# A two-layer decoder trunk on one core: the last feed-forward product by quarter products, and four smaller moves ahead of it

## The chip, the cores and the metric

The kernel runs on one core of a Trainium2 chip. The core has a matrix engine (PE in the profile, with its weight loads shown as PEld), a vector engine (DVE), a scalar engine (ACT), a general engine (POOL) and a queue engine that issues DMAs (SP). Each engine works through its own queue in order and waits on semaphores of the others. The metric is the device time of one execution in microseconds (us); the time of a kernel is the median of its runs.

## The reference

The input is one sequence of 1024 tokens of width 1024. Two layers follow, each a token mixer and a squared-ReLU feed-forward block, and a last RMSNorm:

```
h = modulate(rms_norm(x, norm_mix_g[i]), sh_m, sc_m)
y = recurrent_mixer(h, ...)   if i % 2 == 0   else   pool_mixer(h, ...)
x = x + gt_m[:, None, :] * y
h = modulate(rms_norm(x, norm_ffn_g[i]), sh_f, sc_f)
u = relu(h @ w1[i]);  x = x + gt_f[:, None, :] * ((u * u) @ w2[i])
...
return rms_norm(x, final_norm_g)
```

The six vectors sh, sc and gt of a layer are one product of silu(c) with w_mod, a matrix of 1024 by 6144 for each layer. The feed-forward block is 1024 to 4096 to 1024.

## The kernel before, in words

The activations are held transposed: x[0] holds tokens 0 to 511 and x[1] tokens 512 to 1023, each as eight blocks of 128 features by 512 tokens. A float32 operand is split into a rounded part and a remainder, and a product takes three matrix instructions (`mm3`, lines 188 to 190): high by high, high by low, low by high. One such instruction has 512 columns (a token half) in nearly all of the kernel.

A remainder is made in one of two ways. `split_part` rounds on ACT and subtracts on DVE (line 181). `neg_part` rounds on ACT, negates on ACT, and lets a DMA from POOL's queue add the original on the fly (line 165); the DVE has no part in it. `prepare` does the same for the first weights `w_k` (block q of four holds six of the eight output blocks of the input projection for two of the eight input blocks): q = 0 by DVE, q = 1, 2 and 3 by DMA. The matrix instructions of that stage are on line 401, the small helper `after` on lines 325 and 328 puts its instructions in a written order on ACT, DVE and POOL.

The modulation vectors ("columns" in the following) are made off the matrix engine: a weight block mb of 512 KB is loaded, DVE multiplies it by cond and sums it (`mod_column`, line 207). `drip(n)` traces n such steps; it is called beside the weight loads of the big products, and `drip_until` where a vector is needed.

The feed-forward block goes in eight chunks of 512 hidden features. `f1` makes the squared ReLU of a chunk, `f2` or `f2_fast` multiplies it by w2. `f2_fast` treats the second product of a chunk as a two by two block product over the token halves and two halves of the features and takes seven quarter products for it where eight blocks would be needed. Its operands (t1 to t4 and three of the four u blocks) are made by DVE and ACT in `f1` with fast set; the results are spread over x by DVE (line 773), ACT (777), DVE sums (803, 807) and POOL adds (782). Product 1, 5, 6, 3 and 7 touch both token halves; products 2 and 4 touch x[1] alone. One chunk of layer 0 (chunk 6) is already taken in two visits, five products and later two, with the weight routines `f2_weights_one` and `f2_weights_two`.

The last chunk of layer 1 isn't fast: f1 without the extra operands, then `last_chunk` three times with `f2_block` (eight-block form): tokens 0 to 511, then 512 to 767, then 768 to 1023, the last two with 256 columns. Beside each the squares of finished blocks are summed (`SumSq`: ACT squares, line 262, DVE adds, line 263). `rstd_bcast` turns a sum into 1/rms for every token on all partitions: PE column sums (272), ACT root (275), DVE reciprocal and splits (276 to 280), DVE diagonals (284), PE broadcast (286). The first 512 tokens are scaled and stored by DVE (`final_norm`, 1009), the next 256 by POOL (`mid_norm`, 1024 and 1030), the last 256 by DVE behind a row form of the root (`rstd_row`, 998 to 1001).

The order of the instructions on each engine isn't the order of the text: a scheduler replays the program with its own costs and gives each engine, whenever it comes free, the ready instruction that was traced first. `issue_after` and the helper `after` tie single instructions down. Buffers of a pool are given in the order of the trace: six PSUM banks for products, two for sums, three raw weight buffers, eight split weight buffers, seven temporaries.

Of the kernel before, what the change touches and what calls it, by code (L numbers as in the profile page):

```python
# [15 lines left out]
P = 128  # L16
# [26 lines left out]
def trunk_kernel(ctx, tc, xT, vecs, wmod, w_k, w_in, w_y, w_g, w_out, w_p, w1, w2, outT):  # L43
# [200 lines left out]
    class SumSq:  # L244


        def __init__(self, name, n=H, plan="GGGGGGGG", room=None):
            self.name, self.n, self.plan, self.room = name, n, plan, room
            self.parts = {}
            self.i = 0  # L250

        def add(self, xb):
# [6 lines left out]
            else:  # L259
# [3 lines left out]
                return (G if who == "G" else V).tensor_add(a, a, sq)  # L263

    def rstd_bcast(ss, trace=None):

        nq = ss.n // P
        parts = list(ss.parts.values())
        ps = small_ps()
        for q in range(nq):  # L270
            for pi, a in enumerate(parts):
                PE.matmul(out=ps[:, q:q + 1], lhsT=a[:, q * P:(q + 1) * P], rhs=ones[:, 0:1],  # L272
                          start=(pi == 0), stop=(pi == len(parts) - 1))
        r = mp.tile([P, 4], F32, tag="rstd", name="rstd", bufs=2)
        root = S.activation(r[:, 0:nq], ps[:, 0:nq], AF.Sqrt, bias=eps, scale=1.0 / D)
        V.reciprocal(r[:, 0:nq], r[:, 0:nq])

        rh = mp.tile([P, 4], F32R, tag="rstdh", name="rstdh", bufs=2)[:, 0:nq]
        V.tensor_copy(rh, r[:, 0:nq])
        V.tensor_sub(r[:, 0:nq], r[:, 0:nq], rh.bitcast(F32))  # L280
        bc = small_ps()[:, 0:ss.n]
        for i, part in enumerate((rh.bitcast(F32), r[:, 0:nq])):
            dg = tmp("dg", ss.n).bitcast(F32R)
            last = V.tensor_mul(dg.rearrange("p (q i) -> p q i", i=P), ident[:, None, :].to_broadcast([P, nq, P]),
                                part[:, :, None].to_broadcast([P, nq, P]))
            PE.matmul(out=bc, lhsT=ones_r, rhs=dg, start=(i == 0), stop=(i == 1))
        if trace is not None:
            trace[S], trace[V] = root, last
        return bc
# [57 lines left out]
    def prepare(q, part=0):  # L347
# [14 lines left out]
        if q == 0:  # L362
            return low
        for (dst, _, first), src in zip(low, (w_k[q, :, 0:H], w_k[q, :, H:D], w_k[q, :, D:D + H])):
            after(S.activation, dst, first, AF.Identity, scale=-1.0)
# [7 lines left out]

    low = prepare(0)
    bias_of(0)
# [4 lines left out]
    for k in range(NB):  # L380
# [13 lines left out]
        if k < 3:  # L394
            prepare(k + 1)
        if k + 3 < NB:
# [45 lines left out]

    s1 = SumSq("m01", plan="VVVVVVVV")
    for k in range(NB):
        s1.add(x[1][:, k, :])
    xr = [conv_input(m, ps6[m], 0) for m in range(6)]
    taken = last_traced(S)
# [234 lines left out]
    def f1_jobs(i, c, eng=None):  # L682
        return [partial(lambda j: split_unit(w1[i, c * 4 + j], f"w1_{i}_{c}_{j}", eng, DRIPS[j]), j) for j in range(4)]

# [70 lines left out]

    def f2_fast(i, c, ahead, products=(1, 5, 6, 3, 7, 2, 4), side=iter(())):

# [56 lines left out]
        for r in range(4):  # L814

            for n in products:
                step(r, n)
            next(side, None)

# [37 lines left out]
    ahead = Ahead(jobs(0, 0, 6))  # L857
    f1(0, 0, AB, by_half=True, side=once(lambda: ffn_norm(0, 1, ss[1])), fast="in turn", ahead=ahead)
    drip_until(0, 5)
# [124 lines left out]
    for c in range(2, 7):  # L984
        f1(1, c, AB, fast=True, ahead=ahead)
        f2_fast(1, c, ahead)
    f1(1, 7, AB, ahead=ahead)


    osrc = outT.rearrange("(b p) t -> p b t", p=P)  # L990
    units = [split_unit(w2[1, 7, dp], f"w2_1_7_{dp}") for dp in range(4)]

    def rstd_row(ss):

        parts = list(ss.parts.values())
        ps = small_ps()[:, 0:ss.n]
        for pi, a in enumerate(parts):
            PE.matmul(out=ps, lhsT=ones, rhs=a, start=(pi == 0), stop=(pi == len(parts) - 1))
        r = tmp("rrow", ss.n)
        S.activation(r, ps, AF.Sqrt, bias=eps, scale=1.0 / D)  # L1000
        V.reciprocal(r, r)
        return r

# [8 lines left out]

    def last_chunk(h, t0, n, plan, side=iter(())):
        s = SumSq(f"o{h}{t0}", n, plan)
        for dp in range(4):
            f2_block(1, 7, units[dp], dp, h, s, t0, n)
            next(side, None)
        return s

    def mid_norm():  # L1020

        o = Blocks("omid")
        for k in range(NB):
            G.tensor_scalar_mul(o[:, k, 0:n1], x[1][:, k, 0:n1], vcol("gfin", k))
        yield
        bc = tmp("bc_mid", n1)
        S.copy(bc, rstd_bcast(sb))
        for k0 in range(0, NB, 4):
            for k in range(k0, k0 + 4):
                G.tensor_mul(o[:, k, 0:n1], o[:, k, 0:n1], bc)  # L1030
            nc.sync.dma_start(osrc[:, k0:k0 + 4, H:H + n1], o[:, k0:k0 + 4, 0:n1])
        yield

    n1 = 256
    sa = last_chunk(0, 0, H, "VVVVVVVV")
    sb = last_chunk(1, 0, n1, "VVVVVVVV", once(lambda: final_norm(rstd_bcast(sa), 0, 0, H)))
    sc = last_chunk(1, n1, H - n1, "VVVVVVVX", mid_norm())
    final_norm(rstd_row(sc), 1, n1, H - n1)


# [69 lines left out]
```

## Time and profile before

| | |
|---|---|
| time, median of 3 runs | 1741.27 us (1738.52 to 1742.1) |
| the profiled execution | 1740.37 us, its span 1738.5 us |
| mean granted clock of PE | 0.994 of full speed |
| PE busy | 1690.5 us (97%), 7472 matrix instructions |
| DVE busy | 1358.9 us (78%) |
| ACT busy | 967.2 us (56%) |
| POOL busy | 492.3 us (28%) |
| DMA | 187.33 MB, mean 108 GB/s |

The span runs from the first to the last instruction of the program; the profiled execution lasted 1.9 us longer than its span. Busy time is a sum over one engine's instructions; a busy matrix engine isn't one at its peak. The time that an instruction waited stands in brackets behind it, with what ended the wait.

### The profile page before, as it was taken

To read this page: it belongs to the slowest core of one execution; us is meant where nothing else is said; L and a number is where in the kernel's file an instruction comes from. 1 tells how busy PE (TensorE), PEld (TensorE's weight loads), DVE (VectorE), ACT (ScalarE), POOL (GpSimd) and SP (SyncE) were. 2 spreads that over 40 slices of the span, in tenths; PEclk is the share of its full clock that TensorE was granted. 3 is DMA by queue.
4 is the path that set the end of the run, shared out by engine and by line. 5 is a ranking of instruction groups with operands and counts; after the bars stand their busy time and mean duration, and the time that the engine had idled before them with its cause. 6 is when DMAs were issued, how large, how long until landed. Compare 5 with 4: busy or idle time off the path is not lost.

```text
span 1738.5 us, 20871 instructions
## 1 busy us (share of the span) xinstructions
PE 1690.5 (97%) x7472; PEld 1386.7 (80%) x7472; DVE 1358.9 (78%) x2115; ACT 967.2 (56%) x1660; POOL 492.3 (28%) x419
## 2 busy tenths in 40 slices
PE   6899999999999999999999999999999999999997
PEld 4687778877788888888888888888878787878787
DVE  7897867589898989897973898559696868687847
ACT  6588886555454454545457787745444454545432
POOL 2132343103241414151416333303140405041403
PEclk9999999999999999999999999999999999999999
DMA  9423425642423333332319888841111112120202
GB/s 337 168 93 104 143 85 162 143 119 83 136 72 123 95 99 109 96 117 89 123 37 198 202 192 179 190 118 61 49 59 39 61 38 70 39 69 29 80 6 97
DMA packets 63175, 187.33 MB, mean 108 GB/s; under 512 B 6752, under 2 KB 9184, under 8 KB 63072
## 3 DMA queue, kind: packets, MB, share of 16 engines
q1 hardware_dynamic: 47376, 157.43, 27.6%
q0 software_dynamic: 15696, 28.58, 9.9%
q8 instruction: 58, 0.95, 0.2%
q14 instruction: 45, 0.37, 0.1%
HBM read 181.79 MB, written 4.19 MB: 107 GB/s over the span
## 4 chain that ended last, share of the span: by engine, by line
PE 75%; DVE 10%; issue 3%; ACT 3%; DMA 2%; POOL 1%; DVEq 0%; ACTq 0%; POOLq 0%
PE mm L188 25%; PE mm L189 25%; PE mm L190 25%; DMA mb<-in_wmod 2%; DVE mb L207 1%; DVE xa L773 1%; DVE xb L773 1%; POOL xa L782 1%; DVE xcb L440 1%; DVE w_a_s L181 1%; ACT c L777 0%; DVE gate L530 0%; PE sm L272 0%; DVE w_y L181 0%; DVE w_s L181 0%
## 5 line engine op out<-in xcount | busy, mean ns | idle before, releaser
L188 PE MATMUL mm<-hh,w_w 128*128 128x512 f32 x1024 | 399.7, 390 | 0.9 <-DVE xa L773 0.9
L189 PE MATMUL mm<-hl,w_w 128*128 128x512 f32 x1024 | 399.3, 390 | 0.0
L190 PE MATMUL mm<-hh,w_w 128*128 128x512 f32 x1024 | 399.0, 390 | 0.0
L782 POOL TENSOR_TENSOR xb<-xb,c 128x512 f32<-128x512 f32 x104 | 150.0, 1442 | 625.4 <-ACT c L777 625.2
L188 PEld LDWEIGHTS mm<-hh,w_w 128*128 128x128 f32 x1024 | 192.6, 188 | 43.1 <-DVE xa L773 3.0
L190 PEld LDWEIGHTS mm<-hh,w_w 128*128 128x128 f32 x1024 | 192.6, 188 | 40.2
L189 PEld LDWEIGHTS mm<-hl,w_w 128*128 128x128 f32 x1024 | 192.5, 188 | 39.5
L782 POOL TENSOR_TENSOR xa<-xa,c 128x512 f32<-128x512 f32 x104 | 159.7, 1535 | 145.2 <-ACT c L777 145.2
L777 ACT ACTIVATE c<-c,mod 128x512 f32<-128x512 f32 x104 | 75.3, 724 | 202.6 <-DVE c L803 135.5
L623 ACT ACTIVATE relu<-mm 128x512 f32<-128x512 f32 x128 | 76.2, 596 | 144.7 <-PE mm L190 144.7
L207 DVE SCALAR_TENSOR_TENSOR mb<-mb,cond 128x1024 f32<-128x1024 f32 x80 | 114.5, 1434 | 47.9 <-DMA mb<-in_wmod 47.9
L773 DVE SCALAR_TENSOR_TENSOR xa<-mm,mod,xa 128x512 f32<-128x512 f32 x156 | 113.0, 742 | 25.8 <-POOL xa L782 25.8
L181 DVE TENSOR_TENSOR w_w<-raw_w,w_w 128x512 fp32r<-128x512 f32 x112 | 106.8, 962 | 12.4 <-ACT w_w L180 12.4
L165 POOL DMA_DIRECT2D w_w<-in_w x80 | 70.5, 900 | 151.0 <-ACT w_w L164 120.6
L613 DVE TENSOR_TENSOR u<-usq,u 128x512 fp32r<-128x512 f32 x102 | 70.2, 688 | 16.1 <-ACT u L612 15.8
L188 PE MATMUL mm<-u,w_a_a 128*128 128x512 f32 x200 | 79.1, 396 | 2.3 <-DVE xb L773 1.2
L188 PE MATMUL mm<-u,w_w 128*128 128x512 f32 (+1 forms) x224 | 80.9, 361 | 0.0
L189 PE MATMUL mm<-u,w_w 128*128 128x512 f32 (+1 forms) x224 | 80.5, 360 | 0.1
L190 PE MATMUL mm<-u,w_w 128*128 128x512 f32 (+1 forms) x224 | 80.4, 359 | 0.0
L180 ACT CAST w_w<-raw_w 128x512 fp32r<-128x512 f32 x112 | 65.1, 612 | 25.0 <-PE mm L190 17.3
L189 PE MATMUL mm<-u,w_a_a 128*128 128x512 f32 x200 | 78.0, 390 | 0.0
L190 PE MATMUL mm<-u,w_a_a 128*128 128x512 f32 x200 | 77.9, 389 | 0.0
(326 smaller groups left out, 4030.0 us busy)
## 6 DMA issues: line engine op xcount, KB each, us to landing
raw_w<-in_w SPq DMA_DIRECT2D x148, 512.0 KB, 3.5
mb<-in_wmod SPq DMA_DIRECT2D x80, 512.0 KB, 3.8
w_w<-in_w POOLq DMA_DIRECT2D x80, 256.0 KB, 5.5
mw<-in_wmod SPq DMA_DIRECT2D x16, 512.0 KB, 11.0
raw_in<-in_w_in SPq DMA_DIRECT2D x8, 512.0 KB, 7.0
raw_y<-in_w_y SPq DMA_DIRECT2D x8, 512.0 KB, 3.7
raw_o<-in_w_out SPq DMA_DIRECT2D x8, 512.0 KB, 4.2
outT<-o SPq DMA_DIRECT2D x12, 256.0 KB, 2.2
```

Of the source, the lines that this page charges most:

```text
L165: nc.gpsimd.dma_start(w[:, 1, 0:n], src, accum_op=ALU.add)
L180: S.copy(w[:, 0, 0:n], raw)
L181: (eng or V).tensor_sub(w[:, 1, 0:n], raw, w[:, 0, 0:n].bitcast(F32))
L188: PE.matmul(out=ps, lhsT=wh, rhs=rh, start=first, stop=False)
L189: PE.matmul(out=ps, lhsT=wh, rhs=rl, start=False, stop=False)
L190: PE.matmul(out=ps, lhsT=w[:, 1, c:c + P], rhs=rh, start=False, stop=last)
L207: V.scalar_tensor_tensor(raw, raw, 1.0, cond, op0=ALU.mult, op1=ALU.mult, accum_out=m[:, e:e + 1])
L613: eng.tensor_sub(u[n][:, 1, jj, :], src, u[n][:, 0, jj, :].bitcast(F32))
L623: S.activation(r, ps, AF.Relu)
L773: V.scalar_tensor_tensor(xb, ps, g[:, r + 4 * row:r + 4 * row + 1], xb, op0=ALU.mult, op1=ALU.add)
L777: S.activation(t, src, AF.Identity, scale=g[:, r + 4 * row:r + 4 * row + 1])
L782: G.tensor_add(xb, xb, t)
```

## The change

Five things change.

1. First weights: the remainders of `w_k` blocks 2 and 3 are subtracted by DVE, after the second and fourth step of the stage, and no longer made by a negation on ACT and a DMA from POOL's queue. Block 1 keeps the DMA.
2. First sums: two of the six evictions of the input projection (`conv_input` for m = 0, 1) are traced ahead of the squares of x[1].
3. Columns: the four weight loads of the first feed-forward product trace no column step any more; the steps that are left until mod[0, 5] follow behind `ffn_norm(0, 1)`, two after each block.
4. The last chunk of layer 1: `f1` is fast; five of the seven quarter products are taken first (x[0] is then complete), then products 2 and 4 for the first 256 tokens of x[1] and then for the last 256. x[0] is scaled by the norm's weight on ACT (`scaled_out`), multiplied by 1/rms on POOL and stored (`normed_out`), and so are the first 256 tokens of x[1].
5. Last squares: for the last 256 tokens the squares of the last three blocks aren't added on DVE; their column sums are accumulated in PSUM by PE (`LastSumSq`), and `rstd_bcast` takes the place of `rstd_row`.

```diff
+    class LastSumSq(SumSq):
+        def add(self, xb):
+            if self.i == 0:
+                self.ps = small_ps()
+            if self.plan[self.i] == "V":
+                super().add(xb)
+                if "V" in self.plan[self.i:]:
+                    return
+                a = self.parts["V"]
+            else:
+                a = tmp("sq", self.n)
+                self.i += 1
+                S.activation(a, xb, AF.Square)
+            for q in range(self.n // P):
+                PE.matmul(out=self.ps[:, q:q + 1], lhsT=a[:, q * P:(q + 1) * P], rhs=ones[:, 0:1],
+                          start=(a is self.parts["V"] and q == 0), stop=(self.i == NB), skip_group_check=True)
...
         if q == 0:
             return low
+        if q > 1:
+            return low
         for (dst, _, first), src in zip(low, (w_k[q, :, 0:H], w_k[q, :, H:D], w_k[q, :, D:D + H])):
             after(S.activation, dst, first, AF.Identity, scale=-1.0)
             after(G.dma_start, dst, src, accum_op=ALU.add)
...
         if k < 3:
-            prepare(k + 1)
+            later[k] = prepare(k + 1)
+        for args in {2: later.get(1), 4: later.get(2)}.get(k) or ():
+            after(V.tensor_sub, *args)
...
     s1 = SumSq("m01", plan="VVVVVVVV")
+    xr = [conv_input(m, ps6[m], 0) for m in range(2)]
     for k in range(NB):
         s1.add(x[1][:, k, :])
-    xr = [conv_input(m, ps6[m], 0) for m in range(6)]
+    xr += [conv_input(m, ps6[m], 0) for m in range(2, 6)]
...
     def f1_jobs(i, c, eng=None):
-        return [partial(lambda j: split_unit(w1[i, c * 4 + j], f"w1_{i}_{c}_{j}", eng, DRIPS[j]), j) for j in range(4)]
+        return [partial(lambda j: split_unit(w1[i, c * 4 + j], f"w1_{i}_{c}_{j}", eng, 0 if (i, c) == (0, 0) else DRIPS[j]), j) for j in range(4)]
...
             for n in products:
                 step(r, n)
+            if out_ss is not None:
+                out_ss.add(x[0][:, r, :])
+                out_ss.add(x[0][:, r + 4, :])
...
-    f1(0, 0, AB, by_half=True, side=once(lambda: ffn_norm(0, 1, ss[1])), fast="in turn", ahead=ahead)
+    def first_side():
+        ffn_norm(0, 1, ss[1])
+        yield
+        while (0, 5) not in mod:
+            drip(2)
+            yield
+
+    f1(0, 0, AB, by_half=True, side=first_side(), fast="in turn", ahead=ahead)
...
-    f1(1, 7, AB, ahead=ahead)
+    f1(1, 7, AB, fast=True, ahead=ahead)
...
-    units = [split_unit(w2[1, 7, dp], f"w2_1_7_{dp}") for dp in range(4)]
+    def scaled_out(o, h, t0, n):
+        for k in range(NB):
+            S.activation(o[:, k, 0:n], x[h][:, k, t0:t0 + n], AF.Identity, scale=vcol("gfin", k))
+
+    def normed_out(o, ss, h, t0, n):
+        bc = tmp("bc_out", n)
+        S.copy(bc, rstd_bcast(ss))
+        for k0 in range(0, NB, 4):
+            for k in range(k0, k0 + 4):
+                G.tensor_mul(o[:, k, 0:n], o[:, k, 0:n], bc)
+                if k % 2:
+                    nc.sync.dma_start(osrc[:, k - 1:k + 1, h * H + t0:h * H + t0 + n], o[:, k - 1:k + 1, 0:n])
...
+    def piece(t0, n, plan, side=iter(())):
+        s = (LastSumSq if "X" in plan else SumSq)(f"o{t0}", n, plan)
+        for r in range(4):
+            for row, number in ((0, 2), (1, 4)):
+                w, c0, ops = units[r][number]
+                m, u = r + 4 * row, U[7][ops]
+                ps = acc_mm()[:, 0:n]
+                for k in range(2):
+                    mm3(ps, [w], c0 + k * P, u[:, 0, k, t0:t0 + n], u[:, 1, k, t0:t0 + n], k == 0, k == 1)
+                xb = x[1][:, m, t0:t0 + n]
+                V.scalar_tensor_tensor(xb, ps, mod[1, 5][:, m:m + 1], xb, op0=ALU.mult, op1=ALU.add)
+                s.add(xb)
             next(side, None)
         return s
...
-    sa = last_chunk(0, 0, H, "VVVVVVVV")
-    sb = last_chunk(1, 0, n1, "VVVVVVVV", once(lambda: final_norm(rstd_bcast(sa), 0, 0, H)))
-    sc = last_chunk(1, n1, H - n1, "VVVVVVVX", mid_norm())
-    final_norm(rstd_row(sc), 1, n1, H - n1)
+    sa = SumSq("o0", plan="VVVVVVVV")
+    f2_fast(1, 7, Ahead([partial(f2_weights_one, 1, 7, r, V) for r in range(4)]), (1, 5, 6, 3, 7), out_ss=sa)
+    units = [f2_weights_two(1, 7, r) for r in range(4)]
+    o0, o1 = Blocks("o0"), Blocks("o1")
+    scaled_out(o0, 0, 0, H)
+
+    def first_out():
+        normed_out(o0, sa, 0, 0, H)
         yield
+
+    n1 = 256
+
+    def second_out():
+        scaled_out(o1, 1, 0, n1)
+        yield
+        normed_out(o1, sb, 1, 0, n1)
+        yield
+
+    sb = piece(0, n1, "VVVVVVVV", first_out())
+    sc = piece(n1, H - n1, "VVVVVXXX", second_out())
+    final_norm(rstd_bcast(sc), 1, n1, H - n1)
```

## Rows read from the trace of the kernel before

**Rows 1.** The page, part 4: shares of the chain that ended last, by engine.

```profile
PE 75%; DVE 10%; issue 3%; ACT 3%; DMA 2%; POOL 1%; DVEq 0%; ACTq 0%; POOLq 0%
```

**Rows 2.** Waits of PE, whole span: us in total, times, longest us.

```profile
PE mm L188 <- DVE xa L773: 6.8, 7, 1.0
PE mm L188 <- ACT gelu L545: 6.1, 4, 1.9
...
PE mm L188 <- ACT xr L426: 4.0, 1, 4.0
...
PE sm L272 <- DVE mod L210: 3.9, 1, 3.9
...
PE mm L401 <- DMA k<-in_w_k: 2.1, 2, 1.6
```

**Rows 3.** Busy time by stretch: PE, PEld, DVE, ACT, POOL, granted clock, DMA share, GB/s.

```profile
0.00:57.50 57.50, 43.33 (x158) 31.11 (x158) 43.34 (x79) 36.00 (x60) 9.80 (x45) 1.00 1.01 340
61.80:67.30 5.50, 5.47 (x13) 4.36 (x14) 3.44 (x11) 5.50 (x10) 0.00 (x0) 0.50 0.00 1
65.40:136.40 71.00, 69.72 (x304) 56.48 (x303) 70.06 (x113) 45.22 (x71) 19.68 (x12) 0.99 0.26 82
363.00:367.60 4.60, 4.36 (x17) 3.63 (x18) 3.03 (x9) 0.26 (x1) 0.00 (x0) 0.64 0.31 118
368.50:446.00 77.50, 75.61 (x330) 61.35 (x330) 71.62 (x113) 41.48 (x73) 20.72 (x14) 1.00 0.25 81
897.81:925.01 27.20, 27.20 (x121) 22.52 (x120) 18.92 (x29) 18.73 (x34) 18.54 (x16) 1.00 0.43 106
1636.29:1679.81 43.52, 43.52 (x194) 36.04 (x192) 21.16 (x29) 15.97 (x27) 4.30 (x3) 1.00 0.13 43
1708.31:1719.82 11.51, 11.51 (x98) 11.51 (x97) 11.31 (x23) 3.46 (x9) 5.47 (x6) 1.00 0.49 184
```

**Rows 4.** Timeline of ACT, 55 to 137 us.

```profile
55.97 0.63 ACT L258 ACTIVATE ssqm01V<-xb 128x512 f32<-128x512 f32 x1 [1.42 <-DMA xb<-in_xT]
...
60.06 1.15 ACT L262 ACTIVATE sq<-xb 128x512 f32<-128x512 f32 x2 [0.27 <-DMA xb<-in_xT]
61.11 3.56 ACT L426 ACTIVATE xr<-mm,vec 128x512 f32<-128x512 f32 x6
...
136.44 1.28 ACT L524 ACT_TABLE_LOAD   x1 [7.35 <-DVE coef L498]
```

**Rows 5.** Timeline of DVE, 358 to 363 us.

```profile
358.83 1.23 DVE L207 SCALAR_TENSOR_TENSOR mb<-mb,cond 128x1024 f32<-128x1024 f32 x1 [2.08 <-DMA mb<-in_wmod]
...
362.41 0.69 DVE L263 TENSOR_TENSOR ssq<-ssq,sq 128x512 f32<-128x512 f32 x1
```

**Rows 6.** DMA issues: queue, count, KB each, median us to landing.

```profile
w_k<-in_w_k POOLq DMA_DIRECT2D x6, 256.0 KB, 8.1
```

**Rows 7.** Timeline of POOL behind the five-product stage of layer 0.

```profile
932.77 1.29 POOL L782 TENSOR_TENSOR xb<-xb,c 128x512 f32<-128x512 f32 x1 [0.54 <-ACT c L777]
934.02 1.30 POOL L782 TENSOR_TENSOR xa<-xa,c 128x512 f32<-128x512 f32 x1
```

**Rows 8.** Groups of POOL, 897.81 to 935.5 us: busy us, mean ns, idle before.

```profile
L782 POOL TENSOR_TENSOR xa<-xa,c 128x512 f32<-128x512 f32 x8 | 11.4, 1424 | 3.2 <-ACT c L777 3.2
...
L165 POOL DMA_DIRECT2D w_w<-in_w x8 | 7.7, 1108 | 0.5 <-issue 0.5
```

**Rows 9.** Timeline of DVE from 1701 us to the end.

```profile
1701.77 0.75 DVE L832 SCALAR_TENSOR_TENSOR xa<-mm,mod,xa 128x512 f32<-128x512 f32 x1 [0.52 <-PE mm L190]
...
1708.51 5.36 DVE L1009 SCALAR_TENSOR_TENSOR o<-xa,vec,sm 128x512 f32<-128x512 f32 x8 [0.20 <-PE sm L286]
...
1724.44 1.49 DVE L263 TENSOR_TENSOR ssqo1256V<-ssqo1256V,sq 128x256 f32<-128x256 f32 x2
...
1731.48 3.26 DVE L1009 SCALAR_TENSOR_TENSOR o<-xb,vec,rrow 128x256 f32<-128x256 f32 x8
```

**Rows 10.** Timeline of POOL, last row.

```profile
1724.02 6.11 POOL L1030 TENSOR_TENSOR omid<-omid,bc_mid 128x256 f32<-128x256 f32 x8 [4.79 <-ACT bc_mid L1027]
```

More of the change, by code (lines that the diff above doesn't have):

```diff
@@ L250, in __init__ @@
             self.i = 0
+            self.ps = None
         def add(self, xb):
@@ L268, in rstd_bcast @@
         parts = list(ss.parts.values())
[L269 to L273, printed above, removed]
+        ps = ss.ps
+        if ps is None:
+            ps = small_ps()
+            for q in range(nq):
+                for pi, a in enumerate(parts):
+                    PE.matmul(out=ps[:, q:q + 1], lhsT=a[:, q * P:(q + 1) * P], rhs=ones[:, 0:1],
+                              start=(pi == 0), stop=(pi == len(parts) - 1))
         r = mp.tile([P, 4], F32, tag="rstd", name="rstd", bufs=2)
@@ L372, in normed @@
         after(V.tensor_mul, xn[k], x[0][:, k, :], bc0)
-    low = prepare(0)
+    low, later = prepare(0), {}
     bias_of(0)
@@ L754, in f2_weights_two, with f2_fast @@
         return {2: (w, 0, (1, 0)), 4: (w, 256, "t4")}
-    def f2_fast(i, c, ahead, products=(1, 5, 6, 3, 7, 2, 4), side=iter(())):
+    def f2_fast(i, c, ahead, products=(1, 5, 6, 3, 7, 2, 4), side=iter(()), out_ss=None):
         u, g = U[c], mod[i, 5]
@@ L986, in trunk_kernel @@
         f2_fast(1, c, ahead)
-    f1(1, 7, AB, ahead=ahead)
+    f1(1, 7, AB, fast=True, ahead=ahead)
     osrc = outT.rearrange("(b p) t -> p b t", p=P)
-    units = [split_unit(w2[1, 7, dp], f"w2_1_7_{dp}") for dp in range(4)]
[L993 to L1002, printed above, removed]
+    def scaled_out(o, h, t0, n):
[9 more added lines that the diff above has]
+                    nc.sync.dma_start(osrc[:, k - 1:k + 1, h * H + t0:h * H + t0 + n], o[:, k - 1:k + 1, 0:n])
     def final_norm(bc, h, t0, n):
@@ L1011, in final_norm @@
             nc.sync.dma_start(osrc[:, k0:k0 + per, h * H + t0:h * H + t0 + n], o)
[L1013 to L1016, printed above, removed]
+    def piece(t0, n, plan, side=iter(())):
[10 more added lines that the diff above has]
+                s.add(xb)
             next(side, None)
         return s
[L1020 to L1031, printed above, removed]
+    sa = SumSq("o0", plan="VVVVVVVV")
[5 more added lines that the diff above has]
+        normed_out(o0, sa, 0, 0, H)
         yield
     n1 = 256
-    sa = last_chunk(0, 0, H, "VVVVVVVV")
-    sb = last_chunk(1, 0, n1, "VVVVVVVV", once(lambda: final_norm(rstd_bcast(sa), 0, 0, H)))
-    sc = last_chunk(1, n1, H - n1, "VVVVVVVX", mid_norm())
-    final_norm(rstd_row(sc), 1, n1, H - n1)
+    def second_out():
[6 more added lines that the diff above has]
+    final_norm(rstd_bcast(sc), 1, n1, H - n1)
 def _layout(inputs):
```

## Prediction

> **What bounds the kernel now.** I read the chain that ended last first: three quarters of it is PE [rows 1], so a microsecond saved elsewhere counts only where PE stands still for it, or behind the last product. Next come PE's waits [rows 2]. Of the waits that this change touches the largest are one of 4.0 us on an xr eviction, one of 3.9 us on line 272's sums behind a column's DVE step, and 2.1 us in two pieces on weights w_k. Then the windows [rows 3], for what else these stops cost. After the first, 13 matrix instructions take 5.47 us of PE, 0.42 each, at a granted clock of 0.50 (the lower of the two levels); in the stage of f1(1, 7) one takes 43.52 / 192 = 0.227. The standstill thus costs 4.0 and then 13 x (0.42 - 0.227) = 2.5: 6.5 us. After the second the clock is 0.64 over 4.60 us, so (1 - 0.64) x 4.60 = 1.7 is lost: 5.6 with the wait. The same windows show what follows. Behind the first stop DVE is busy for 70.06 of 71.0 us, behind the second for 71.62 of 77.5. PE too is busy there, but its largest sum of waits in the whole span is on DVE's xa evictions, 6.8 us [rows 2]. Whoever starts PE earlier in these stretches must ask whether DVE can follow.
>
> The end is another matter. The span ends at 1738.5; the last rows of DVE and POOL [rows 9, 10] carry what follows the last product.
>
> **First weights.** Six negations on ACT and six DMAs of 256 KB from POOL's queue go [rows 6]. The six subtractions that replace them are 128x512 operations of DVE with two inputs in SBUF; by the addition of that shape, 0.69 [rows 5], they cost 6 x 0.69 = 4.1 us. DVE has 57.5 - 43.34 = 14 us free there [rows 3], and that room hides them; without it they cost up to 4.1. The DMA engines have none free: share 1.01 at 340 GB/s [rows 3]. 1.5 MB less is 1.5 / 0.34 = 4.6 us less in their queues, but the added block then reaches its place by DVE, behind the loads. Of PE's 2.1 us, the piece of 1.6 belongs to the second block used, which keeps its DMA; the other 0.5 can go. Bounds -0.5 and +1.0 (two subtractions, 1.4, between a normalised block and its split, less a part of that wait); I take 0.
>
> **First sums.** Two banks are emptied before the squares. In the trace ACT waits four times for blocks of x[1], from 1.42 down to 0.27 us, some 2.1 in all, then does the squares, and starts the six evictions at 61.11, in 3.56 [rows 4]: 0.59 each. Two of these ahead free two banks, and PE can go on. If nothing else held it the gain would be the whole 6.5. But the stage that follows, from 65.4 to 136.4, is DVE's, 1% short of full, and ACT stands for 7.35 us at its end waiting for DVE's coef [rows 3, 4]. PE's lead would run into that wait. What really moves is DVE's start, by what the first squares and evictions gain from ACT's idle 2.1. I take -2; bounds -0.3 (the last of the four waits) and -6.5.
>
> **Columns.** Four steps leave the weight loads of the first feed-forward product. One lies at 358.83, after 2.08 of waiting for its weights, and the norm's sums stand behind it on DVE [rows 5]; PE's 3.9 is that. Without it, -5.6 for PE. The steps don't vanish: 4 x 1.23 = 4.9 us of DVE return behind ffn_norm(0, 1), in the stretch from 368.5 to 446 where DVE has 77.5 - 71.62 = 5.9 left [rows 3]. They fit on paper, not in each place where PE waits for an eviction. Bounds -5.6 (all fit) and 0 (4.9 returns, and some waiting for mb with it); I take -2, nearer to the full DVE.
>
> **Last chunk, by PE.** Before: 96 instructions of 512 columns at 0.227 and 192 of 256 columns at 0.12 (11.51 / 96 [rows 3]), 21.8 + 23.0 = 44.8 us from 1679.81. After: five products are 120 of 512, which layer 0's five-product stage shows as 27.20 without a gap, and products 2 and 4 are 2 x 48 of 256, 11.5: 38.7. If PE set the end, -6.1, an end at 1732.4.
>
> **Last chunk, by POOL.** I hold that POOL sets it. The work on x[0] now waits for the last of the spreading adds, on POOL. The five-product stage of layer 0 ends on PE at 925.01; its last POOL add ends at 934.02 + 1.30 = 935.32 [rows 3, 7], 10.3 late. There POOL also issues eight weight DMAs, 7.7 us, beside eight xa adds of 11.4 [rows 8]; here four remainders are DVE's and four DMAs stay. Bounds 5 (the lag without half of those issues, and the last add with its evictions still behind PE) and 10.3; I take 7.5. From 1679.81 + 27.20 = 1707.0 that gives x[0] complete at 1714.5. Before, from x[0] complete (1701.77 + 0.75 = 1702.5) to its first scaled output (1708.51) it took 6.0 [rows 9]; the copy of 1/rms on ACT adds 0.6, by an xr eviction [rows 4]. POOL's products start at 1721.1: eight of 512 columns at 1.29 to 1.30, as its adds [rows 7], 10.3 us, then eight of 256, 6.11 [rows 10]. That ends at 1737.5. Before, DVE scaled x[0] in 5.36 [rows 9]; the same work on POOL takes nearly twice as long, and the second batch stands behind the first in the queue.
>
> Beside DVE the products may be slower. POOL's adds of 1.29 average 1.424 [rows 8], and two 256-column additions on DVE take 1.49 while POOL multiplies, 0.75 each, longer than the 0.69 of one with twice the columns [rows 5, 9, 10]. So 16 x 0.13 = 2.1 more is what the mean shows; with bounds 0 and 3 I take 1.5: 1739.0. Behind the last scaled output before comes 1738.5 - (1731.48 + 3.26) = 3.8 of store and end [rows 9]; that gives 1742.8, or +4.3. With all low bounds (5, 0) it is 1738.8, +0.3; with the high ones (10.3, 3) 1747.1, +8.6.
>
> On these rows bears a rule of the Trainium skill, page "SBUF — State Buffer", section "Who interferes with whom": DVE and GpSimd (POOL) share a pair of ports, which an operation of DVE with two SBUF inputs, or one of GpSimd, holds alone from its start to its end while the other stands. By that rule each POOL product could also stand behind one whole DVE operation with two SBUF inputs; the slow DVE additions above agree with it, and it speaks against moving the scaling to POOL. By it the price could reach 16 x 0.69 = 11 us where I take 1.5; without it, with products at 1.29 throughout, the sum would be 1.5 lower.
>
> **Last squares.** DVE loses three additions of 256 columns, two of which took 1.49 [rows 9]: -1.5 at best. The column form of the root brings a path like the 6.0 above in place of the row form: some +2 at worst. Both lie on the path of the last 256 tokens, which by PE ends near 1732.4 and by POOL's queue at 1742.8; the 10 us between hide them, so 0. If that cover went, -1.5 to +2.
>
> **Sum.** 0 - 2 - 2 + 4.3 = +0.3 on a span of 1738.5. The profiled execution lasted 1740.37, 0.9 below the median of 1741.27, so the forecast is 1741.5 against that median: no change that can be told. About 0.2%, 3.5 us, is what a measurement of this kernel can tell from none.
>
> **Rivals.**
> (a) Faster: DVE isn't the bound behind the two stops. For it speaks that PE is busy 69.72 of 71.0 and 75.61 of 77.5 there [rows 3], so it is nearly as full, and that DVE's work can be late without PE waiting as long as a bank is free. Against it, the 7.35 behind coef. Then PE keeps most of its gain: -6 - 5.3 + 4.3 is -7, about 1734; with POOL's low bound 1730.
> (b) Slower: POOL's queue at the end. The lag stays at layer 0's 10.3 and its products stand behind DVE's, +8.6, and the front gives only 0.3 to 3: +5.6 to +8.3, about 1748. It decides once POOL's last product would end after 1740.2 on the old trace's clock (3.8 behind it, less 2 from the front, is 1742.0, 3.5 above the old span); I put it at 1739.0. For it speaks that ACT, which now spreads products, squares them and scales x[0], is late too.
> (c) The first two evictions are still issued behind the squares, because the order on ACT is the scheduler's and not the text's; then that part does nothing, and the sum is +2.3, 1743.6. For it: ACT's squares are ready in time where the banks aren't. Against it: an instruction traced first goes first when both are ready.
> (d) At the end PE sets the time, POOL's products being hidden: POOL's lag would have to be under 1; no row shows so little.
>
> **How the numbers follow.** My forecast has 0.27, its own range 1738 to 1745; (c) has 0.10, and both mean no change. (a) has 0.31, with (d) 0.33; (b) has 0.30. The likeliest single case gives 1741.5. To leave out no more than 2 in 10 the range reaches to (a) below, with the front's bounds nearly whole, 1732, and to the upper end of (b), 1749. Faster 0.33, same 0.37, slower 0.30.
>
> **What would show it.** In the changed trace PE's 4.0 us on xr and 3.9 on line 272 should be gone or below 1, and the clock at 1.00 through 61.8 to 67.3 and 363 to 367.6. If the end of the stretch to 136.4 moves by only 2 us while its start moves by more, DVE is shown as its bound; if it moves by 6, (a) is. At 446 the same question stands for the columns. The last chunk should show PE's last product some 39 us behind its start, and POOL's 16 products in line 1.3 and 0.76 us long without a pause, the last of them 3 to 4 us ahead of the end. If DVE's last outputs end later than POOL's, my step on POOL is wrong, and the end is to be sought on PE's path. A pause of POOL between its two batches, or a first product before 1716 in terms of the old clock, would make it too dear.

## The result and the profile after

The change makes the kernel slower: 1756.32 us, median of 5 runs (1755.76 to 1760.61), against 1741.27 (1738.52 to 1743.9); the ratio is 1.0092, 95% interval 1.0081 to 1.0103. The forecast was 1741.5 with a range up to 1749. The profiled execution is the longest of the five (span 1758.8), so the traces differ by 20.3 us where the medians differ by 15.1. The start of the last chunk also moves from run to run (1676.3 to 1682.2 in the traces with the same front), so for the tail the times below are counted from the first product of that chunk: 1679.81 before, 1681.54 after.

The chain that ended last has less PE and more DVE than before [rows 1]:

```profile
PE 68%; DVE 18%; issue 4%; ACT 4%; DMA 4%; POOL 2%; DVEq 0%; SPq 0%; ACTq 0%; POOLq 0%
```

PE's waits after (us in total, times, longest), to be read beside [rows 2]:

```profile
PE sm L294 <- DVE ssqo0V L264: 10.9, 2, 8.3
PE mm L188 <- DVE xa L800: 8.6, 9, 1.2
...
PE mm L188 <- ACT hh L317: 6.0, 1, 6.0
...
PE mm L188 <- ACT c L804: 2.9, 1, 2.9
```

The 4.0 on the eviction and the 3.9 on the sums of line 272 are gone, as foreseen, and the clock is 1.00 from 61.8 to 67.3; but over 60 to 82 it is 0.84. In their place stand one wait of 6.0 on the normalised x[1], more time on xa evictions (8.6 for 6.8), and, new and largest, 10.9 on the squares of the outputs.

The last chunk in three windows (busy time of PE, PEld, DVE, ACT and POOL, granted clock, DMA share, GB/s). First the kernel before: products of x[0], the other products, what follows the last product.

```profile
1679.81:1701.60 21.79, 21.79 (x98) 18.05 (x97) 11.35 (x16) 6.16 (x10) 0.00 (x0) 1.00 0.01 2
1701.60:1726.87 25.27, 25.27 (x209) 24.97 (x207) 21.18 (x48) 7.44 (x19) 10.54 (x12) 1.00 0.22 84
1726.87:1738.50 11.63, 1.40 (x4) 0.59 (x4) 6.03 (x11) 0.89 (x2) 3.26 (x5) 0.76 0.53 180
```

The changed kernel: five products, products 2 and 4, what follows.

```profile
1681.50:1709.07 27.57, 27.54 (x121) 22.45 (x121) 21.33 (x29) 21.88 (x39) 17.27 (x15) 1.00 0.29 58
1709.07:1732.50 23.43, 17.89 (x107) 17.22 (x105) 17.86 (x29) 13.51 (x30) 10.44 (x9) 0.78 0.08 12
1732.50:1758.80 26.30, 6.31 (x25) 5.55 (x24) 16.11 (x31) 3.93 (x12) 13.54 (x14) 0.59 0.45 160
```

The five products take the forecast 27. Products 2 and 4 take 23.4 where 11.5 was forecast: PE is busy for 17.9, at a granted clock of 0.78. Behind the last product come 26.3 us where 11.6 were. In all 77.3 for 58.7.

What PE does between its products there (start, length, and the wait ahead of it):

```profile
1712.88 0.38 PE L188 MATMUL mm<-ut,w_a_a 128*128 128x256 f32 x1 [2.94 <-ACT c L804]
...
1717.82 0.28 PE L189 MATMUL mm<-ut,w_a_a 128*128 128x256 f32 x1
1720.70 1.84 PE L294 MATMUL sm<-ones,ssqo0V 128*128 128x1 f32 x8 [2.60 <-DVE ssqo0V L264]
1722.40 0.56 PE L190 MATMUL mm<-ut,w_a_a 128*128 128x256 f32 x1
...
1727.46 0.39 PE L308 MATMUL sm<-dg,ones_r 128*128 128x512 f32 x1
...
1740.78 0.98 PE L294 MATMUL sm<-ones,ssqo0V 128*128 128x1 f32 x4 [8.28 <-DVE ssqo0V L264]
```

The sums of x[0]'s squares have a fixed place in PE's queue, inside a product (its third instruction follows at 1722.40). PE stands there because x[0] isn't complete. POOL's rows say when it is, and what comes next:

```profile
1717.76 1.26 POOL L809 TENSOR_TENSOR xa<-xa,c 128x512 f32<-128x512 f32 x1
1729.19 11.16 POOL L1040 TENSOR_TENSOR o<-o,bc_out 128x512 f32<-128x512 f32 x8 [10.18 <-ACT bc_out L1037]
1744.96 5.68 POOL L1040 TENSOR_TENSOR o<-o,bc_out 128x256 f32<-128x256 f32 x8 [4.61 <-ACT bc_out L1037]
```

x[0] is complete at 1719.02, 37.5 after the start of the chunk (1681.54), where before it was 22.7 (1702.5, [rows 9]). From there to POOL's first product it is 10.2 us. And while POOL multiplies, DVE's groups from 1728 to 1742 (busy, mean ns of one, idle) read:

```profile
L264 DVE TENSOR_TENSOR ssqo0V<-ssqo0V,sq 128x256 f32<-128x256 f32 x6 | 7.6, 1262 | 1.0 <-ACT sq L263 1.0
L264 DVE TENSOR_TENSOR ssqo256V<-ssqo256V,sq 128x256 f32<-128x256 f32 x3 | 3.4, 1124 | 0.0
L1064 DVE SCALAR_TENSOR_TENSOR xb<-mm,mod,xb 128x256 f32<-128x256 f32 x5 | 2.4, 474 | 0.7 <-PE mm L190 0.7
```

Nine additions of squares take 11.0 us, 1.2 each in the mean; PE's 8.3 above is the wait for the last of the six on ssqo0V. The updates of line 1064 beside them, with one operand in PSUM, are not longer than elsewhere.

### The profile page after: what moved, and what is told of

The parts are those of the page before. It is cut to its first block, busy times and chain, and to the rows that moved or that the text cites. A ratio compares the mean times of both kernels' runs of the same rounds, so it can differ in the third digit from the quotient of the medians.

```text
span 1758.8 us, 20853 instructions
## 1 busy us (share of the span) xinstructions
PE 1692.8 (96%) x7414; PEld 1387.0 (79%) x7414; DVE 1388.9 (79%) x2157; ACT 994.5 (57%) x1713; POOL 517.0 (29%) x433
## 4 chain that ended last, share of the span: by engine, by line
PE 68%; DVE 18%; issue 4%; ACT 4%; DMA 4%; POOL 2%; DVEq 0%; SPq 0%; ACTq 0%; POOLq 0%
PE mm L188 23%; PE mm L189 22%; PE mm L190 22%; DMA mb<-in_wmod 3%; DVE mb L207 2%; DVE xa L800 1%; POOL xa L809 1%; DVE xb L800 1%; DVE xca L466 1%; DVE xcb L466 1%; DVE w_a_s L181 1%; DVE nt L316 1%; DVE mw L350 1%; PE sm L294 1%; DVE hl L318 0%
## 5 line engine op out<-in xcount | busy, mean ns | idle before, releaser
L809 POOL TENSOR_TENSOR xb<-xb,c 128x512 f32<-128x512 f32 x112 | 160.7, 1435 | 669.7 <-ACT c L804 669.5
L809 POOL TENSOR_TENSOR xa<-xa,c 128x512 f32<-128x512 f32 x112 | 172.4, 1539 | 149.6 <-ACT c L804 149.6
L804 ACT ACTIVATE c<-c,mod 128x512 f32<-128x512 f32 x112 | 81.0, 724 | 204.9 <-DVE c L830 135.4
L800 DVE SCALAR_TENSOR_TENSOR xa<-mm,mod,xa 128x512 f32<-128x512 f32 x168 | 121.9, 742 | 27.7 <-POOL xa L809 27.7
L181 DVE TENSOR_TENSOR w_w<-raw_w,w_w 128x512 fp32r<-128x512 f32 x104 | 101.9, 990 | 9.1 <-ACT w_w L180 9.1
L188 PE MATMUL mm<-u,w_a_a 128*128 128x512 f32 (+1 forms) x216 | 85.1, 394 | 5.3 <-DVE xa L800 3.3
L189 PE MATMUL mm<-u,w_a_a 128*128 128x512 f32 (+1 forms) x216 | 83.5, 387 | 0.0
L190 PE MATMUL mm<-u,w_a_a 128*128 128x512 f32 (+1 forms) x216 | 83.3, 386 | 0.0
L800 DVE SCALAR_TENSOR_TENSOR xb<-mm,mod,xb 128x512 f32<-128x512 f32 x104 | 77.0, 740 | 0.9 <-PE mm L190 0.5
L180 ACT CAST w_w<-raw_w 128x512 fp32r<-128x512 f32 x104 | 60.3, 612 | 28.0 <-PE mm L190 15.4
L189 PE MATMUL mm<-ut,w_a_s 128*128 128x512 f32 x192 | 74.8, 390 | 0.4 <-DVE ut L640 0.4
L188 PE MATMUL mm<-ut,w_a_s 128*128 128x512 f32 x192 | 75.0, 390 | 0.2 <-ACT ut L639 0.2
## 6 DMA issues: line engine op xcount, KB each, us to landing
mw<-in_wmod SPq DMA_DIRECT2D x16, 512.0 KB, 10.8
```

The costliest lines, as they stand in the source:

```text
L180: S.copy(w[:, 0, 0:n], raw)
L181: (eng or V).tensor_sub(w[:, 1, 0:n], raw, w[:, 0, 0:n].bitcast(F32))
L188: PE.matmul(out=ps, lhsT=wh, rhs=rh, start=first, stop=False)
L189: PE.matmul(out=ps, lhsT=wh, rhs=rl, start=False, stop=False)
L190: PE.matmul(out=ps, lhsT=w[:, 1, c:c + P], rhs=rh, start=False, stop=last)
L800: V.scalar_tensor_tensor(xb, ps, g[:, r + 4 * row:r + 4 * row + 1], xb, op0=ALU.mult, op1=ALU.add)
```

## The experiments

Medians, and the ratio to the kernel before with its interval:

| run | median us | ratio (95%) |
|---|---|---|
| e1 parts 1 to 3 alone | 1739.96 | 0.9993 (0.9984 to 1.0002) |
| e2 parts 4 and 5 alone | 1758.39 | 1.0101 (1.0087 to 1.0115) |
| e3 DVE multiplies | 1757.19 | 1.0089 (1.0077 to 1.0102) |
| e4 squares summed by PE | 1755.11 | 1.0077 (1.0064 to 1.0091) |
| e5 no norm of x[0] | 1741.99 | 1.0004 (0.9995 to 1.0013) |
| e6 its norm later | 1753.99 | 1.0074 (1.0059 to 1.0089) |
| e7 later and on DVE | 1753.94 | 1.0073 (1.0056 to 1.0090) |
| e8 row form of the root | 1756.37 | 1.0084 (1.0069 to 1.0099) |
| e9 its sums earlier | 1750.54 | 1.0058 (1.0043 to 1.0073) |
| e10 first sums alone | 1740.56 | 0.9996 (0.9987 to 1.0004) |
| e11 columns alone | 1740.27 | 0.9995 (0.9985 to 1.0004) |
| e12 first weights alone | 1740.01 | 0.9994 (0.9985 to 1.0003) |
| e13 norm without products | 1748.49 | 1.0045 (1.0030 to 1.0060) |
| e14 products without norm | 1751.40 | 1.0062 (1.0047 to 1.0077) |
| e15 squares of x[0] late | 1758.55 | 1.0101 (1.0084 to 1.0118) |

Four of them (e5, e9, e13 and e14) leave out a part of the work on tokens 0 to 511 and so store other values for them; they are diagnoses and no candidates.

**Where the loss lies.** e1 is the changed kernel with the last chunk of before, e2 the kernel before with the changed last chunk.

> The changed kernel with the last chunk and its squares as before: parts 1 to 3 alone. Theory A (the whole loss is in the last chunk): the changed trace stands 1.7 us behind at the start of that stage, so about 1743, a ratio of 1.000 to 1.002. Rival B (the front loses several us in ordinary runs, the one trace is a lucky one): 1746 or more. Rival C (as forecast): a gain of 4, about 1737.

> The kernel before with parts 4 and 5 alone (the last chunk by quarter products and the last squares). Theory A: +13 to +17, that is 1754 to 1758, nearly all of the changed kernel's loss. Rival B: +8 or less, 1749 at most. My forecast for this part was +4.3, 1745.6.

The whole loss is in the last chunk: e2 has 1.0101 and e1 has 0.9993. Theory A's 1743 for e1, taken from one trace, was too high. No gain shows in front, and its interval, down to 0.9984 (-2.8 us), leaves out the -4 of the forecast.

**POOL or DVE for the products.** My first theory was that POOL's products hold up DVE's additions, and that this is the loss.

```diff
-                G.tensor_mul(o[:, k, 0:n], o[:, k, 0:n], bc)
+                V.tensor_mul(o[:, k, 0:n], o[:, k, 0:n], bc)
```

> The changed kernel with the sixteen products that scale the outputs on DVE and no longer on POOL. Theory T1 (POOL's products hold up DVE's additions of squares, one by one): the additions go back from 1.1 to 1.5 us each to 0.41, the eight products take 0.69 each on DVE, the second sums come 5 to 8 us earlier: 1747 to 1751. Rival T3 (the end is set by PE's queue, where sums stand between products): the last product on PE stays where it is and at most 3 us are won: 1753 or more. Rival T2 (POOL is only slow): as T1 in time, but DVE's additions are seen as short in both traces, which the next kernel tells apart.

The theory failed: 1757.19, no better. DVE's groups in e3, 1726 to 1736, show why:

```profile
L1040 DVE TENSOR_TENSOR o<-o,bc_out 128x512 f32<-128x512 f32 x8 | 4.9, 688 | 0.7 <-ACT bc_out L1037 0.7
L264 DVE TENSOR_TENSOR ssqo0V<-ssqo0V,sq 128x256 f32<-128x256 f32 x6 | 2.5, 419 | 0.0
```

The additions are back at 0.42, so POOL did stretch them. But now the eight products stand in DVE's queue ahead of them. That it is POOL's doing is right; that this alone is the loss is not. In e4 the additions go, and PE sums the squares of every block:

```diff
...
-    sb = piece(0, n1, "VVVVVVVV", first_out())
-    sc = piece(n1, H - n1, "VVVVVXXX", second_out())
+    sb = piece(0, n1, "XXXXXXXX", first_out())
+    sc = piece(n1, H - n1, "XXXXXXXX", second_out())
```

> The changed kernel with POOL's products as they are, but no addition of squares on DVE for the last 512 tokens: PE sums each block's squares by columns into PSUM. T1: with no two-input addition to hold up, the second sums follow the last product within some 4 us, POOL's second batch starts right behind its first: 1748 to 1751. T2 (POOL's sixteen products in a row set the end whatever DVE does): POOL's end moves by its 4.6 us of idle time at most, 1752 to 1754. T3 (PE's queue): sixteen more small column sums on PE for each piece make it slower, 1757 or more.

1755.11 lies between the cases T2 and T3. The additions' wait is gone, but the small sums stand in PE's queue between products, and the last product ends 60.1 us after the start of the chunk, not 51.0. Both moves shift the price to another queue.

**Leaving the norm of x[0] out.**

```diff
-        normed_out(o0, sa, 0, 0, H)
+        for k in range(0, NB, 2):
+            nc.sync.dma_start(osrc[:, k:k + 2, 0:H], o0[:, k:k + 2, 0:H])
```

> The changed kernel without the norm of tokens 0 to 511: their blocks are stored as ACT's scaling leaves them, so that root, broadcast and POOL's eight products of 512 columns are left out (a diagnosis, with that part of the output not normalised). Theory T4 (the norm of x[0] stands in the queues of PE, ACT and DVE ahead of the work on the last 512 tokens, is late, and holds it all up): PE's last product comes some 8 us earlier and the end 12 to 16 earlier, 1741 to 1745. Rival T5 (the last path, from the last product through the squares to the store, is long by itself): 8 us from PE at most and not more, 1748 to 1750. Rival T6 (the price lies ahead of this, in the five products with their late POOL adds): 1753 or more.

1741.99: 14.3 us come back, nearly the whole loss. Its windows (as above):

```profile
1676.25:1703.78 27.53, 27.50 (x122) 22.45 (x120) 21.29 (x28) 21.88 (x39) 17.27 (x15) 1.00 0.37 96
1703.78:1722.93 19.15, 14.52 (x101) 13.53 (x99) 17.40 (x35) 14.04 (x33) 7.16 (x6) 0.91 0.25 70
1722.93:1737.80 14.87, 3.84 (x20) 2.82 (x20) 8.02 (x21) 1.87 (x6) 6.12 (x8) 0.67 0.42 141
```

Even so the chunk takes 61.6 us, 2.9 more than before: products 2 and 4 still take 19.2, with a wait of 2.9 on ACT's eviction at their start and DVE busy for 17.4 of 19.15. The seven quarter products save nothing here even with x[0]'s norm free.

**Norm and products apart.** e13 keeps sums, root, broadcast and copy, and drops the eight products; e14 drops the chain and multiplies by another tile.

```diff
-        normed_out(o0, sa, 0, 0, H)
+        bc = tmp("bc_out", H)                                        # e13
+        S.copy(bc, rstd_bcast(sa))
...
+        for k in range(NB):                                          # e14
+            G.tensor_mul(o0[:, k, 0:H], o0[:, k, 0:H], x[0][:, k, 0:H])
...
```

> The changed kernel with the sums, root, broadcast and copy of x[0]'s norm kept, but without POOL's eight products by it (a diagnosis: tokens 0 to 511 are stored not normalised). Theory P (the products, by the port they hold, are most of what is left): DVE's additions take 0.41 throughout and follow PE's last product by 2 to 3 us; 8 to 11 us faster than the changed kernel, 1745 to 1748. Rival Q (the chain in the queues of PE and ACT is most of it): 4 us at most, 1752 or more.

> The changed kernel without sums, root, broadcast and copy of x[0]'s norm, but with POOL's eight products, now by x[0] itself (a diagnosis: other numbers are stored for tokens 0 to 511). The products begin as soon as POOL's adds allow, about 1718 to 1720, and run beside PE's products. Theory P with L (they cost by standing beside DVE's additions, the less the earlier they start): 4 to 8 us faster than the changed kernel, 1748 to 1752. Rival Q: 10 us or more, 1746 at most.

Put as a loss against the kernel before (the ratio less 1, times 1741): 16.0 us with both, 7.8 with the chain (sums, root, broadcast, copy) alone, 10.8 with the products alone, 0.7 with neither. From e5 over e13 to the changed kernel, the chain adds 7.1 and the products 8.2. Neither theory stands as it was put: e13 is just above the 1748 of P, and Q's 1752 and 1746 are both missed. Each part is about half. In e13 DVE's same nine additions (1724 to 1731) are short:

```profile
L264 DVE TENSOR_TENSOR ssqo0V<-ssqo0V,sq 128x256 f32<-128x256 f32 x6 | 2.5, 418 | 1.0 <-ACT sq L263 1.0
L264 DVE TENSOR_TENSOR ssqo256V<-ssqo256V,sq 128x256 f32<-128x256 f32 x3 | 1.3, 418 | 0.0
```

3.8 us for 11.0: 7.2 of the products' 8.2. e14's 10.8 isn't the same work. Its products stand among POOL's adds, and there they hold up one of DVE's additions, of 128x512, much longer:

```profile
1697.56 7.05 DVE L264 TENSOR_TENSOR ssqo0V<-ssqo0V,sq 128x512 f32<-128x512 f32 x1 [0.70 <-ACT sq L263]
```

Such an addition takes 0.68 in the changed kernel when POOL stands still (1702.86), and 2.45 beside POOL's adds (1699.82). In e14 POOL works without a pause from 1697.89 to 1704.05: two adds, two products and a DMA's issue. Behind it the eviction of xa is late, PE waits 3.7 and later 1.6 for it, and the five products take 35.2 us and not 27.6.

**Later, or earlier.** e6 traces x[0]'s norm one piece later; e7 also scales x[0] on DVE; e9 starts the norm earlier, from the sums of six blocks out of eight.

```diff
-    scaled_out(o0, 0, 0, H)                      # e7 only
...
-        normed_out(o0, sa, 0, 0, H)              # e7 only
+        final_norm(rstd_bcast(sa), 0, 0, H)      # e7 only
...
+    def late():
+        yield from first_out()
+        yield from second_out()
+
-    sb = piece(0, n1, "VVVVVVVV", first_out())
-    sc = piece(n1, H - n1, "VVVVVXXX", second_out())
+    sb = piece(0, n1, "VVVVVVVV")
+    sc = piece(n1, H - n1, "VVVVVXXX", late())
```

> The changed kernel with the norm of x[0] traced behind the first step of the last piece instead of the first step of the piece before, and the norm of the middle tokens behind it; the same instructions in another order. T4: PE's products run through, the last one 5 to 8 us earlier than in the changed kernel, and the end 4 to 9 us earlier, 1747 to 1752, although POOL starts no earlier. T5 and T6: within 2 us of the changed kernel's 1756.

> As the kernel with the late norm, but x[0] scaled and stored by DVE from PSUM, as in the kernel before, with neither ACT's scaling nor POOL's products for it; POOL keeps the middle tokens. T4 with T1: 2 to 5 us better than the late norm alone, 1743 to 1749. If POOL's products of x[0] don't matter once the norm is late: equal to it.

Late, PE's products do run through (the last one ends 45.7 and 46.5 us after the start, not 51.0), but only some 2.3 us are won, less than the 4 of T4: PE then waits 5.1 (e6) and 7.6 (e7) for the additions of squares, behind POOL's products in the one, behind DVE's own scaling in the other. The two tie, as my second expectation of e7 had it, but not for its reason: each meets a wait of its own.

```diff
-            if out_ss is not None:
+            if out_ss is not None and r < 3:
...
-    sa = SumSq("o0", plan="VVVVVVVV")
+    sa = SumSq("o0", plan="VVVVVV")
```

> The changed kernel with the squares of x[0] summed over six of its eight blocks, those of the first three steps (a diagnosis: the 1/rms of tokens 0 to 511 is not the reference's). Root, broadcast, scaling and POOL's products all remain; they only start one step, some 7 to 9 us, earlier. Theory L (x[0] is late, and its norm has no cover left): POOL's first product starts about 1720 in place of 1729, and the end comes 6 to 10 us earlier, 1746 to 1750. Rival W (the amount of this work, or the port that POOL holds, sets the end whenever it starts): 3 us at most, 1753 or more.

POOL's products and DVE's groups (1718 to 1731) in e9:

```profile
1718.59 11.19 POOL L1040 TENSOR_TENSOR o<-o,bc_out 128x512 f32<-128x512 f32 x8 [4.28 <-ACT bc_out L1037]
```

```profile
L264 DVE TENSOR_TENSOR ssqo0V<-ssqo0V,sq 128x256 f32<-128x256 f32 x6 | 7.2, 1198 | 0.2 <-ACT sq L263 0.2
```

The first product stands 41.8 us after the start of the chunk (start 1676.83) for 47.7 in the changed kernel, 5.9 earlier; the median is 5.8 lower, just under what theory L expected, while the additions are as long as ever. So here a later start of x[0]'s norm passes into the time nearly one to one. It isn't that start alone: x[0] itself is complete as late as before, 37.5, but two additions of squares and PE's wait of 2.6 are gone too.

**Why x[0] is late.** e15 traces its squares behind the five products.

```diff
-            if out_ss is not None:
+            next(side, None)
+        if out_ss is not None:
+            for r in range(4):
                 out_ss.add(x[0][:, r, :])
                 out_ss.add(x[0][:, r + 4, :])
-            next(side, None)
```

> The changed kernel with the squares of x[0] traced behind the whole five-product stage, so that they don't stand in ACT's queue ahead of evictions. Theory: PE's wait of 2.9 us on an eviction by ACT is gone, x[0] is complete 1 to 3 us earlier, but its sums begin later; the end moves by -3 to +2, 1753 to 1758. Rival (the squares in ACT's queue cause the lag of x[0] and its norm starts earlier for it): 1750 or less.

1758.55, no gain, and just above the range I gave: the wait on ACT's c is gone, but one of 2.6 on xa stands in its place, and PE's wait for the second squares grows from 8.3 to 10.9. x[0] is complete 38.3 after the start of the chunk, no earlier than the 37.5 of the changed kernel, so the place of the squares in ACT's queue isn't what makes it late. Nor is ACT's scaling of x[0]: in e7, which has none, it is 39.5.

**The last squares.** e8 takes back part 5.

```diff
...
-    sc = piece(n1, H - n1, "VVVVVXXX", second_out())
-    final_norm(rstd_bcast(sc), 1, n1, H - n1)
+    sc = piece(n1, H - n1, "VVVVVVVX", second_out())
+    final_norm(rstd_row(sc), 1, n1, H - n1)
```

> The changed kernel with part 5 undone: the squares of the last piece summed on DVE but for the last one, and the row form of the root. In the changed trace the column sums take 3.6 us and what follows to the first output 2.6, on the path that ends the kernel. T5: 1 to 3 us faster, 1753 to 1755. My forecast (cover hides either form): equal, 1755 to 1757.5. If the DVE additions that come back are held up by POOL: slower, up to 1759.

Equal, as forecast, but not for the reason given: the path that I held to be covered is the one that ends the kernel. From the last addition to the first output the column form takes 6.2 us after the change (1745.97 to 1752.22), the row form 4.5 in e8 (1744.54 to 1749.01); the additions that it needs stand against that.

**The front, part by part.** Each of the three takes the lines of its part from the diff of the change into the kernel before, and nothing else (e10 the two evictions, e11 the columns, e12 the subtractions).

> The kernel before with part 2 alone: two evictions traced ahead of the squares of x[1]. By the changed trace PE's wait of 4.0 on an eviction turns into one of 6.0 on the norm of x[1]: 1738.5 to 1741.5, a gain of 0 to 2.5. My forecast for it was -2. Rival (PE keeps the gain): 1735.

> The kernel before with part 3 alone. By the changed trace PE gains 2.0 up to 442 and loses 3.2 to DVE's evictions from 488 to 524: 1741 to 1743. My forecast for it was -2, 1739. Rival (all fits): 1736.

> The kernel before with part 1 alone. My forecast was 0 with bounds of -0.5 and +1.0; the changed trace stands 1.0 behind at the last of these weights, before the next stop takes it up: 1740 to 1742, which is the same as before. Rival (the DMA queue is freed and x[1] comes 4 us earlier): 1737.

None can be told from no change. In e10, PE's wait and DVE's share of the 17 us behind it are plain:

```profile
PE mm L188 <- ACT hh L295: 6.1, 1, 6.1
```

```profile
65.00:82.00 17.00, 10.94 (x38) 8.44 (x39) 17.00 (x25) 7.73 (x14) 7.06 (x4) 0.82 0.20 63
```

The 4.0 on the eviction has shrunk to 0.5; PE then runs up against x[1]'s normalised blocks, with DVE busy for all 17.00 us. In e11 the 3.9 on the sums is gone, and in the same norm PE now waits 2.5 for DVE's diagonals (dg, line 284), where the kernel before doesn't wait:

```profile
PE sm L286 <- DVE dg L284: 5.0, 3, 2.5
```

Before, all its waits on dg were 2.5 in two places. PE's waits on xa are 8.2 in nine places for 6.8 in seven [rows 2], but that shows little: e10 and e12, which leave the columns alone, have 7.6.

## Why the prediction was wrong

- **First weights, first sums, columns.** 0, -2 and -2 were forecast. Alone, none can be told from no change (the intervals reach down to 0.9987 and 0.9985 for the two that were to gain, some -2.3 and -2.6, so -2 for one of them isn't excluded); together -1.2 with -2.8 as the bound, so -4 was too much. The argument was right as to what would happen: DVE is the bound behind the first stop, as e10's window shows, and behind the second PE's gain runs into 2.5 of waiting for DVE in the same norm. The clock's loss has moved too and isn't gone: 0.82 over e10's 17 us. Rival (a), that PE keeps its lead, is refuted. ([rows 6] count the six w_k transfers of all three blocks; the six that go are four of these and two of k, so the sum stands.)
- **Last chunk, by PE.** The term "five products 27.2" came out at 27.57; the term "products 2 and 4, 11.5" was the first to fail: 23.43. I took durations from a stretch in which nothing interrupts PE. Of the 11.9 more, 2.9 are the wait on ACT's eviction, 2.6 the wait on x[0]'s sums and 1.8 those sums, 7.3 together; the other 4.6 are mostly the lower clock. It was granted at 0.50, the lower level, from 1720.7 to 1727.1, behind 2.8 us in which PE was busy for 0.2, and at 0.66 in the mean from 1712.88 to 1717.9, behind the wait of 2.9. 256-column products start 0.21 apart from 1713.8 to 1716.8 and from 1722.76 to 1727.0, and 0.12 apart from 1727.2; 35 of them so far apart are 3.2 us.
- **Last chunk, by POOL: x[0] late.** The forecast put x[0] complete 34.7 us after the start of the chunk; it was 37.5, its last add 9.9 behind PE's five products, near the upper bound of 10.3 and not at 7.5. Four weight DMAs less did not bring the lag down. In the last step the three engines hand one block to and fro: ACT's c waits 0.78 and 0.76 for DVE's sums (1714.22, 1715.70), DVE's second sum 0.79 for ACT (1714.97), POOL's adds 0.81 and 0.20 for ACT (1715.02, 1716.50). That this exchange paces the lag is read from these waits; no version changed it.
- **From x[0] complete to POOL's first product.** 6.0 + 0.6 was taken from the kernel before; it took 10.2. Sums, root and broadcast share the queues: the sums run at the lower clock (1.84 at 0.50; before, 1.01 at 1.00), DVE's splits stand between updates of line 1064, the broadcast's two instructions have their places among products (1727.46, 1728.04). POOL's start is thus 6.4 late (47.7 after the start of the chunk; 1721.1 meant 41.3).
- **The step that decided: "with bounds 0 and 3 I take 1.5", and the cover of the last 256 tokens.** I counted the shared port as a price on POOL's products. They take 11.16 for eight, 0.8 over the forecast 10.3. The price fell on DVE: nine additions at 1.2 and not 0.42, and e13 gives 7.2 of it back. I treated POOL's outputs and the path of the last tokens as two paths, the second hidden by 10 us. They are one: the sums of the middle tokens wait for the additions, POOL's second batch for those sums (its idle 4.61), and the squares of the last tokens stand behind that batch's copy on ACT. DVE's outputs, not POOL's, end the kernel (1755.4 and 3.4 of store; POOL is through at 1750.6), which the prediction named as the sign that its step on POOL is wrong. The sum shows the sizes. For the chunk +4.3 was forecast and +18.6 measured (77.3 for 58.7), 14.3 more: x[0] 2.8 later, 3.6 more to POOL's first product, 1.1 less for POOL's two batches than 10.3 + 6.11 + 1.5, 4.6 of idle between them, and 8.2 behind POOL's end in place of 3.8.
- **Rival (b)** had the sign, the place and the lag, 10.3, and fell short by the same step: 1748 for 1756.

The Trainium skill, page "SBUF — State Buffer", section "Who interferes with whom", says that a DVE instruction with two SBUF inputs contends with a GpSimd (POOL) instruction that reads SBUF, that one with at most one SBUF input doesn't, and that the port pair is an exclusive lock. The trace agrees, in the direction that I left out: DVE's additions last 1.09 to 1.48 while POOL multiplies, and 0.41 for the last, when POOL is through, while its updates with an operand in PSUM stay at 0.47.

What stays open: how the lag of 10 behind five products could be shortened. e15 shows that it isn't the squares, and e7 that it isn't ACT's scaling; the adds on POOL themselves weren't moved. Nor did a run part the chain's 7.1 by its steps. No version ran that beats the kernel before beyond its interval.

## What to carry to other kernels

When products are saved at the end of a kernel, look first whether the first half of the output is still finished early enough for its norm and its store to run under products that are left. Here x[0] was complete 14.8 us later, its norm then cost some 15 us (7.1 by its chain, 8.2 by its products), and even with that norm left out the chunk was no shorter (61.6 for 58.7). A chain of small steps that is late can cost twice in in-order queues: it is late itself, and what stands behind its places in the queues of PE, ACT and DVE is late with it. When work goes to an engine that shares a port with another, price the operations of the other engine that run at the same time, and not only by one each (e14's 7.05), and look whether they are on the path.

## What the runs showed of the hardware

- A 128x256 addition on DVE from two SBUF operands takes 0.42 us alone (e13, e3) and 1.2 us in the mean while POOL multiplies 128x512 blocks; POOL's products go from 1.24 (9.90 / 8 in e4, which has none of these additions) to 1.40 (11.16 / 8). Beside several POOL operations in a row one addition of 128x512, 0.68 alone, took 7.05 (e14).
- Sixteen column sums of one column each take 3.6 us (1746.03 to 1749.6), 0.22 each, at a granted clock of 0.50, the lower level. That is as much as a product instruction of 512 columns takes in the five-product stage at 1.00 (27.57 / 121 = 0.228). At 1.00, the kernel before has eight such sums in 0.9 us, 0.11 each (1704.44 to 1705.32).
